# Seven block products for eight in the gate and up products of one token group, with two of the four weight sums made by DMA

## The chip, the cores and the metric

The kernel runs on one core of one Trainium2 chip. The metric is the device time of one execution in microseconds (us), as the median of several runs. Three runs of the kernel before gave 1436.48 us as the median (1433.87 to 1438.87).

## The reference, cut to what matters

One layer of a streaming encoder is computed for 1056 tokens: 1024 of a prompt and 32 of a running stream, with the same weights. Everything is float32. The part that the change touches is the feed-forward half:

```python
h = x * (1 + sc2) + sh2                                  # x: 1056 x 1024, after the first layer norm
y = (jax.nn.silu(h @ w_gate) * (h @ w_up)) @ w_down      # w_gate, w_up: 1024 x 2816; w_down: 2816 x 1024
x = _layer_norm(ALPHA * x + (1 + g2) * y, ln2_g, ln2_b)
```

## The kernel before, in words

Tokens lie along the free dimension, features along the partitions. The tokens are cut into two groups: group 0 has 512 and group 1 has 544 (`GN`). Each group is cut again into two halves (`MM`): 256 and 256, or 272 and 272. The 2816 hidden features are 22 tiles of 128; the 1024 input features are 8 blocks of 128 (`KT`).

Matrix products keep float32 accuracy by splitting both operands into a high and a low part of type float32r. `weights` (line 91) loads a block of weights of 128x1024 into a raw buffer, ScalarE casts it to the high part (line 102), and VectorE subtracts to get the low part (line 103). `gemm` (line 108) then runs three matmuls for each of the 8 input blocks: high by high (line 114), high by low (line 115) and low by high (line 116). There are three raw buffers (`RAW`), three for the high parts and three for the low parts (`WB`); the weights of all stages share them.

`up` (line 972) makes one tile of 128 hidden features for one group. It loads the tile's gate weights and its up weights, and for each half of the group runs the gate product and the up product, 24 matmuls each. Then ScalarE makes the sigmoid with three functions (lines 987 to 989), VectorE multiplies (lines 990 and 991), and the result is split into high and low (lines 992 and 993). One such tile of group 1 has 96 matmuls of 272 columns.

`down` (line 1011) takes a group of three or four such tiles (`GROUPS`) and adds their product with w_down into the residual `z`, for 8 blocks of 128 output features and two halves; `sublayer_end` (line 915) does the addition on VectorE (line 923). One tile more than the group has is made ahead of each `down`, so that the last tile's elementwise work is covered.

The order in `run` around the change: the tiles of group 0 come first, and among the last of them group 1's first layer norm is interleaved (`ln1`, line 930, which also writes the operand of group 1: `hh[1]` and `hl[1]`, high and low). Then `down(0, last)`, and `ln1_res` (line 947) on GpSimd. Then group 1: tiles 0 to 3, the last layer norm of group 0 (`ln2`, line 1025), `down` of tiles 0 to 2, tiles 4 to 6, `down`, tiles 7 to 10, `down`, and so on. The last group of tiles (19 to 21, with 18 made before) is done half by half: tiles 19, 20, 21 of the first half, `down`, `ln2`, and then the same for the second half, with the weights of the three tiles loaded and split a second time.

All loads and stores go through SyncE's queue in one order. The order of the instructions on each engine is fixed when the program is built, by a scheduler that follows the order of the code and what it expects to be ready.

Of the kernel before, what the change touches and what calls it, by code (L numbers as in the profile page):

```python
# [7 lines left out]
F32 = mybir.dt.float32  # L8
# [55 lines left out]
def f(ap):  # L64
    return ap.bitcast(F32)


class Kernel:
# [13 lines left out]
        return pool.tile(shape, dt, tag=tag, name=f"{self.phase}_{tag}_{self.n}", **kw)  # L82

    def load(self, out, in_):
        return self.nc.sync.dma_start(out, in_)

    def store(self, out, in_):
        self.nc.sync.dma_start(out, in_)
# [782 lines left out]

    def operand(self, c, pool):

        self.hh[c], self.hl[c] = ({a: self.t(pool, [P, KT, b - a], F32R, f"{x}{a}", 1) for a, b in MM[c]}
                                  for x in ("ah", "al"))

    def wo_mix(self, c, ks):
        self.phase = f"wo{c}"
# [51 lines left out]
    def ln1(self, c, st, a, b):  # L930
        self.phase = f"lna{c}"
        nc, z, hh, hl, sl = self.nc, self.z[c], self.hh[c][a], self.hl[c][a], slice(a, b)
        r, e = self.ln_stats(st, sl)
        for k in range(KT):
            yield
            self.phase = f"lna{c}"
            zk = z[:, k, sl]
            nc.vector.tensor_tensor(zk, zk, r, ALU.mult)
# [33 lines left out]
    def up(self, c, j, act, pool, cuts):  # L972
        self.phase = f"up{c}"
        nc, hh, hl = self.nc, self.hh[c], self.hl[c]
        ah, al = act[j] = [self.t(pool, [P, GN[c]], F32R, x, 5) for x in ("acth", "actl")]
        w = [self.weights(self.d["w_gu"][2 * j + i], KT, P) for i in range(2)]
        for a, b in cuts:
            ps = []
            for i in range(2):
                p = self.t((self.pg, self.pu)[i], [P, 512], F32, self.utag[i])[:, :b - a]  # L980
                self.gemm(p, w[i], slice(0, P), lambda k: hh[a][:, k], lambda k: hl[a][:, k])
                ps.append(p)
                if i == 0:
                    yield
                    self.phase = f"up{c}"
            s = self.t(self.p2, [P, 272], F32, "sil", 4)[:, :b - a]
            nc.scalar.activation(s, ps[0], AF.Exp, scale=-1.0)
            nc.scalar.activation(s, s, AF.Ln, bias=self.one)
            nc.scalar.activation(s, s, AF.Exp, scale=-1.0)
            nc.vector.tensor_tensor(s, ps[0], s, ALU.mult)  # L990
            nc.vector.tensor_tensor(s, ps[1], s, ALU.mult)
            nc.scalar.copy(ah[:, a:b], s)
            nc.vector.tensor_tensor(al[:, a:b], s, f(ah[:, a:b]), ALU.subtract)
            yield
            self.phase = f"up{c}"

    def last_weights(self, dst, units):

# [54 lines left out]
    def run(self):  # L1053
# [11 lines left out]
        self.dsf = t([8, 2, PAST + NS], "dsf")  # L1065
        self.dM = t([4, 9, P], "dM")
        self.dd0 = t([4, 9], "dd0")
        self.dmix = [t([P, KT, GN[c]], f"dmix{c}") for c in range(2)]
        self.pg = self.pool("pg", NB[0], space=PSUM)
        self.pt = self.pool("pt", NB[1], space=PSUM)  # L1070
# [124 lines left out]
        for g, (j0, nj) in enumerate(GROUPS):  # L1195
            if g == WOB:
                s4.close()
                s3.close()
                self.pu, self.utag = self.pool("pu", 3, space=PSUM), "gu"
                pb = self.pb = self.pool("pb", side="right")  # L1200
                weave(self.up(0, j0 + 1, act, pa, MM[0]))
                self.operand(1, pb)
                with tc.issue_after(self.lastz.ins):
                    self.wo_mix(1, self.KORDER)
                stb = self.ln_begin(nc.gpsimd)
                self.wo(1, stb, MM[1], nc.vector, pb)
                self.operand(1, pb)

                def norm():
                    for a, b in MM[1]:  # L1210
                        yield from self.ln1(1, stb, a, b)

                def fill():
                    for j in range(j0 + 2, j0 + nj):
                        yield from self.up(0, j, act, pa, MM[0])
# [12 lines left out]
        st.update(pivot=False, sum=True)  # L1228
        self.down(0, last, act, MM[0], st)
        self.ln1_res(1)  # L1230
        s5.close()
        pa = self.pool("pa1")
        act = {}
        for g, (j0, nj) in enumerate(GROUPS[:-1]):
            for j in range(j0 + (g > 0), j0 + nj + 1):
                weave(self.up(1, j, act, pa, MM[1]))
            if g == 0:
                for a, b in LN[0]:
                    self.ln2(0, st, a, b, "vpvvpvvp", "aaaaaaaa")
            st = self.ln_begin(nc.gpsimd, sum=False) if g == last - 1 else None  # L1240
            self.down(1, g, act, MM[1], st)
        st.update(pivot=False, sum=True, order=(4, 5, 6, 7, 0, 1, 2, 3))
        j0, nj = GROUPS[-1]

        n = nj * 256
        t = self.t(self.pz, [P, 4, n], F32R, "z0", 1)
        w = self.last_weights(((t[:, 0], t[:, 1]), (t[:, 2], t[:, 3])), (2, 3))
        act2 = dict(act)
        for half, (a, b) in enumerate(LN[1]):
            for j in range(j0 + 1 + (half and UPF), j0 + nj):  # L1250
                weave(self.up(1, j, (act, act2)[half], pa, ((a, b),)))
            if half == 0:
                h, l = (self.t(pb, [P, KT, b - a], F32R, f"{x}{a}", 1).rearrange("p k n -> p (k n)") for x in ("ah", "al"))
                for j in range(j0 + 1, j0 + 1 + UPF):
                    weave(self.up(1, j, act2, pa, (LN[1][1],)))
# [18 lines left out]
def _layout(inputs):  # L1274
# [21 lines left out]
    for n in ("ln1_g", "ln1_b", "ln2_g", "ln2_b"):  # L1296
# [16 lines left out]
    a["w_gu"] = units(np.stack([g["w_gate"][0].reshape(1024, 22, 128), g["w_up"][0].reshape(1024, 22, 128)],  # L1313
                               axis=2).reshape(1024, 5632), 128)
# [48 lines left out]
```

## Time and profile before

| | |
|---|---|
| median of 3 runs | 1436.48 us |
| the profiled execution | 1436.1 us, of which the span is 1434.3 us |
| TensorE (PE) busy | 1385.6 us, 97% of the span |
| VectorE (DVE) busy | 960.7 us, 67% |
| ScalarE (ACT) busy | 641.3 us, 45% |
| GpSimd (POOL) busy | 254.3 us, 18% |
| DMA | 205.49 MB on the one queue that the kernel uses |

PE's busy time is the time in which at least one matmul was in flight. Group 1's tiles and what follows them take the last 420 us of the span or so; the work of group 0 and of the mixers lies ahead of them.

### The profile page before, as it was taken

To read this page: it belongs to the slowest core of one execution; us is meant where nothing else is said; L and a number is where in the kernel's file an instruction comes from. 1 tells how busy PE (TensorE), PEld (TensorE's weight loads), DVE (VectorE), ACT (ScalarE), POOL (GpSimd) and SP (SyncE) were. 2 spreads that over 40 slices of the span, in tenths; PEclk is the share of its full clock that TensorE was granted. 3 is DMA by queue.
4 is the path that set the end of the run, shared out by engine and by line. 5 is a ranking of instruction groups with operands and counts; after the bars stand their busy time and mean duration, and the time that the engine had idled before them with its cause. 6 is when DMAs were issued, how large, how long until landed. Compare 5 with 4: busy or idle time off the path is not lost.

```text
span 1434.3 us, 28877 instructions
## 1 busy us (share of the span) xinstructions
PE 1385.6 (97%) x11141; PEld 1336.3 (93%) x11141; DVE 960.7 (67%) x2220; ACT 641.3 (45%) x1405; POOL 254.3 (18%) x295
## 2 busy tenths in 40 slices
PE   7999999999999899999999999999999999999994
PEld 4899988989899889999999998999999999999994
DVE  5558655678688777687767765668857545454676
ACT  3323244434445564546555353436745342424353
POOL 0103100043157300000000002254500000000433
PEclk9999999999999999999999999999999999999997
DMA  9754678565654755443443533522224222222431
GB/s 359 253 210 128 200 206 259 160 197 168 224 176 151 215 161 178 115 145 120 126 139 104 101 104 67 196 89 74 100 73 153 89 89 89 89 89 89 133 104 63
DMA packets 120867, 207.35 MB, mean 145 GB/s; under 512 B 21380, under 2 KB 76300, under 8 KB 120728
## 3 DMA queue, kind: packets, MB, share of 16 engines
q1 hardware_dynamic: 120728, 205.49, 45.9%
q8 instruction: 88, 1.44, 0.4%
q14 instruction: 51, 0.42, 0.1%
HBM read 173.78 MB, written 31.66 MB: 143 GB/s over the span
## 4 chain that ended last, share of the span: by engine, by line
PE 82%; DMA 7%; DVE 6%; ACT 1%; issue 1%; SPq 1%; POOL 1%; DVEq 0%; ACTq 0%; POOLq 0%
PE up_g L115 8%; PE up_g L116 8%; PE up_g L114 8%; PE dn_g L114 4%; PE dn_g L115 4%; PE dn_g L116 4%; PE up_u L116 3%; PE up_u L115 3%; PE up_u L114 3%; PE tm_g L279 2%; PE tm_g L280 2%; PE tm_g L281 2%; PE fox_t L729 2%; PE wo_g L114 2%; PE wo_g L115 2%; PE wo_g L116 2%
## 5 line engine op out<-in xcount | busy, mean ns | idle before, releaser
L114 PE MATMUL up_g<-wo_ah,up_whi 128*128 128x256 f32 (+1 forms) x1008 | 288.8, 287 | 3.4 <-ACT lna_tmp L942 3.3
L115 PE MATMUL up_g<-wo_al,up_whi 128*128 128x256 f32 (+1 forms) x1008 | 290.4, 288 | 0.4 <-DVE wo_al L945 0.4
L116 PE MATMUL up_g<-wo_ah,up_wlo 128*128 128x256 f32 (+1 forms) x1008 | 289.4, 287 | 0.0
L114 PEld LDWEIGHTS up_g<-wo_ah,up_whi 128*128 128x128 f32 x1008 | 191.4, 190 | 4.9 <-ACT wo_ah L944 3.5
L115 PEld LDWEIGHTS up_g<-wo_al,up_whi 128*128 128x128 f32 x1008 | 191.6, 190 | 1.3 <-DVE wo_al L945 0.7
L116 PEld LDWEIGHTS up_g<-wo_ah,up_wlo 128*128 128x128 f32 x1008 | 191.3, 190 | 0.4 <-DVE up_wlo L103 0.2
L102 ACT CAST up_whi<-up_raw 128x1024 fp32r<-128x1024 f32 x94 | 98.5, 1047 | 143.1 <-PE dn_u L115 53.8
L103 DVE TENSOR_TENSOR up_wlo<-up_raw,up_whi 128x1024 fp32r<-128x1024 f32 x94 | 121.1, 1288 | 61.0 <-ACT up_whi L102 60.7
L114 PE MATMUL dn_g<-up_acth,dn_whi 128*128 128x256 f32 (+1 forms) x464 | 133.8, 289 | 2.4 <-DVE mlstm_z L923 2.4
L115 PE MATMUL dn_g<-up_actl,dn_whi 128*128 128x256 f32 (+1 forms) x464 | 132.3, 286 | 0.0
L116 PE MATMUL dn_g<-up_acth,dn_wlo 128*128 128x256 f32 (+1 forms) x464 | 132.1, 285 | 0.0
L116 PE MATMUL up_u<-wo_ah,up_wlo 128*128 128x272 f32 (+1 forms) x400 | 115.4, 289 | 0.0
L114 PE MATMUL up_u<-wo_ah,up_whi 128*128 128x272 f32 (+1 forms) x400 | 114.9, 287 | 0.0
L115 PE MATMUL up_u<-wo_al,up_whi 128*128 128x272 f32 (+1 forms) x400 | 114.5, 286 | 0.0
L280 PE MATMUL tm_g<-tm_wlo,start_h1h 128*128 128x256 f32 (+1 forms) x384 | 111.3, 291 | 0.0
L281 PE MATMUL tm_g<-tm_whi,start_h1l 128*128 128x256 f32 (+1 forms) x384 | 111.0, 290 | 0.0
L279 PE MATMUL tm_g<-tm_whi,start_h1h 128*128 128x256 f32 (+1 forms) x384 | 110.3, 289 | 0.2 <-ACT tm_mixs L630 0.2
L114 PE MATMUL fm_g<-start_h1h,fm_whi 128*128 128x256 f32 (+2 forms) x344 | 102.7, 304 | 5.5 <-ACT fm_whi L102 1.9
L115 PE MATMUL fm_g<-start_h1l,fm_whi 128*128 128x256 f32 (+2 forms) x344 | 102.5, 298 | 0.1
L116 PE MATMUL fm_g<-start_h1h,fm_wlo 128*128 128x256 f32 (+2 forms) x344 | 101.4, 296 | 0.0
L114 PEld LDWEIGHTS dn_g<-up_acth,dn_whi 128*128 128x128 f32 x464 | 87.7, 189 | 3.3 <-DVE mlstm_z L923 3.0
L115 PEld LDWEIGHTS dn_g<-up_actl,dn_whi 128*128 128x128 f32 x464 | 87.8, 189 | 0.4
(447 smaller groups left out, 3806.2 us busy)
## 6 DMA issues: line engine op xcount, KB each, us to landing
up_raw<-w_gu SPq DMA_DIRECT2D x94, 512.0 KB
dn_raw<-w_dn SPq DMA_DIRECT2D x30, 512.0 KB
ada_late<-w_ada SPq DMA_DIRECT2D x24, 512.0 KB
wo_raw<-w_o SPq DMA_DIRECT2D x24, 512.0 KB
ada_araw<-w_ada SPq DMA_DIRECT2D x16, 512.0 KB
fm_raw<-w_in_f SPq DMA_DIRECT2D x16, 512.0 KB
tm_raw<-w_in SPq DMA_DIRECT2D x12, 512.0 KB
dn_raw<-w_dn SPq DMA_DIRECT2D x16, 384.0 KB
```

What stands on the lines that cost most here:

```text
L102: nc.scalar.copy(hi[:, :w], raw[:, :w])
L103: (eng or nc.vector).tensor_tensor(lo[:, :w], raw[:, :w], f(hi[:, :w]), ALU.subtract)
L114: nc.tensor.matmul(ps, hi, xh(k), start=start and k == 0, stop=False)
L115: nc.tensor.matmul(ps, hi, xl(k), start=False, stop=False)
L116: nc.tensor.matmul(ps, lo, xh(k), start=False, stop=stop and k == n - 1)
L279: nc.tensor.matmul(ps[:, :ncol], xh, hi, start=k == 0, stop=False)
L280: nc.tensor.matmul(ps[:, :ncol], xh, lo, start=False, stop=False)
L281: nc.tensor.matmul(ps[:, :ncol], xl, hi, start=False, stop=k == 7)
L729: nc.tensor.transpose(ps[:, y * P:(y + 1) * P], probs[y][:, b * P:(b + 1) * P], self.ident)
```

## The change

Group 1's tiles 4 to 20, seventeen of them, are made by a new function `sup` in the place of `up`. It treats the tile's product as a product of 2x2 blocks: gate and up by the lower and upper four input blocks on the side of the weights, the lower and upper four input blocks by the two halves of 272 tokens on the side of the operand. Seven block products with sums of blocks (the form of Strassen and Winograd) give the four results that eight block products gave. Each block product has four input blocks, so 12 matmuls.

- The sums on the operand's side are made once, by `sup_operand`, during group 1's tiles 0 and 1. It reads the operand back from DRAM, where `ln1` now stores it, and writes four sums of 128x4x272, split into high and low, into the buffers that held group 0's operand.
- Of the four sums of weights, two are made in DRAM by `sums`: SyncE copies the lower up block twice into a buffer `dp`, and one call later a DMA issued from GpSimd adds the lower gate block and the upper up block to it. There is one call of `sums` ahead of each of the last three tiles of group 0 or so, and one per tile of group 1 up to tile 15, so that a tile's sums are made some six tiles ahead of their use. The other two sums are two additions of 128x512 on VectorE in `sup`.
- A tile of `sup` loads 512 KB of gate weights, 512 KB of sums and 256 KB of up weights. It splits the gate weights, the two sums of its own, the two sums from DRAM, and the upper up block.
- The last layer norm of group 0 is divided: one half after tile 2, the other after tile 3.
- Tiles 19 and 20 are no longer done half by half; only tile 21 is.
- The buffers of the sigmoid are two of 544 columns for four of 272.

```diff
@@ load, ln1, up
     def load(self, out, in_):
-        return self.nc.sync.dma_start(out, in_)
+        self.lastload = self.nc.sync.dma_start(out, in_)
+        return self.lastload
...
+            if c:
+                self.store(self.dh[:, k, sl], h)
             nc.scalar.copy(hh[:, k], h)
             nc.vector.tensor_tensor(hl[:, k], h, f(hh[:, k]), ALU.subtract)
...
-            s = self.t(self.p2, [P, 272], F32, "sil", 4)[:, :b - a]
+            if a == cuts[0][0]:
+                sil = self.t(self.p2, [P, 544], F32, "sil", 2)
+            s = sil[:, a:b]
@@ new
+    def sums(self):
+        i = self.nsum
+        self.nsum += 1
+        blocks = lambda j: self.d["w_gu"][j].rearrange("p (b n) -> p b n", b=4)
+        if i < FF:
+            with self.tc.issue_after(self.lastload.ins):
+                self.store(self.dp[i], blocks(i)[:, 2:3].to_broadcast([P, 2, 512]))
+        if SJ <= i - 1 < FF:
+            self.nc.gpsimd.dma_start(self.dp[i - 1], blocks(i - 1)[:, 0:4:3], accum_op=ALU.add)
+
+    def sup_operand(self, ks):
...
+        for k in ks:
...
+            self.load(x, self.dh[:, k])
+            self.load(y, self.dh[:, k + 4])
+            tt(y[:, b], y[:, b], x[:, b], ALU.subtract)
+            tt(x[:, b], x[:, a], x[:, b], ALU.subtract)
+            tt(x[:, a], y[:, b], x[:, a], ALU.add)
+            tt(y[:, a], x[:, a], y[:, a], ALU.subtract)
+            for z, (h, l) in zip((x, y), self.T):
+                nc.scalar.copy(h[:, k], z)
+                tt(l[:, k], z, f(h[:, k]), ALU.subtract)
+            yield
+
+    def sup(self, j, act, pool):
...
+        raw = [self.t(self.wp, [P, 1056], F32, "raw", RAW)[:, :n] for n in (1024, 1024, 512)]
+        self.load(raw[0], self.d["w_gu"][j][:, :1024])
+        self.load(raw[1], self.dp[j].rearrange("p b n -> p (b n)"))
+        self.load(raw[2], self.d["w_gu"][j][:, 1536:])
...
+        w1 = big(raw[0])
+        tt(raw[0][:, lo], raw[0][:, lo], raw[1][:, hi], ALU.add)
+        tt(raw[0][:, hi], raw[0][:, hi], raw[0][:, lo], ALU.add)
+        w3 = big(raw[0])
+        w4 = big(raw[1])
+        w2 = split(*(self.t(self.px, [P, 544], F32R, x, 1)[:, :512] for x in ("w2h", "w2l")), raw[2])
...
+        nc.scalar.copy(u1, prod(w1[:4], own(0, 0)))
+        tt(x[:, a], prod(w1[4:], own(0, 4)), u1, ALU.add)
+        tt(uv[:, a], u1, prod(w3[:4], com(0)), ALU.subtract)
+        tt(uv[:, b], prod(w4[4:], com(1)), uv[:, a], ALU.add)
+        tt(x[:, b], prod(w3[4:], own(272, 4)), uv[:, b], ALU.add)
+        s = self.t(self.p2, [P, 544], F32, "sil", 2)
+        nc.scalar.activation(s, x, AF.Exp, scale=-1.0)
+        nc.scalar.activation(s, s, AF.Ln, bias=self.one)
+        nc.scalar.activation(s, s, AF.Exp, scale=-1.0)
+        tt(s, x, s, ALU.mult)
+        two = lambda y: y.rearrange("p (t n) -> p t n", t=2)
+        tt(two(c), prod(w4[:4], com(3)).unsqueeze(1).to_broadcast([P, 2, 272]), two(uv), ALU.add)
+        tt(c[:, a], prod(w2, com(2)), c[:, a], ALU.add)
+        nc.vector.scalar_tensor_tensor(c, c, -1.0, s, ALU.mult, ALU.mult)
+        nc.scalar.copy(ah, c)
+        tt(al, c, f(ah), ALU.subtract)
@@ run, group 1
+        operand = self.sup_operand(range(4))
+        for g, (j0, nj) in enumerate(GROUPS):
+            for j in range(j0 + (g > 0), min(j0 + nj + (g < last), FF - TS)):
+                if self.nsum <= FF:
+                    self.sums()
+                if j >= SJ:
+                    self.sup(j, act, pa)
+                    continue
+                if j == 2:
+                    weave(operand)
+                for _ in self.up(1, j, act, pa, MM[1]):
+                    if j < 2:
+                        next(operand, None)
+                if j >= 2:
+                    a, b = LN[0][j - 2]
+                    self.ln2(0, self.st0, a, b, "vpvvpvvp", "aaaaaaaa")
...
         for half, (a, b) in enumerate(LN[1]):
-            for j in range(j0 + 1 + (half and UPF), j0 + nj):
+            for j in range(FF - TS, FF):
                 weave(self.up(1, j, (act, act2)[half], pa, ((a, b),)))
```

`FF` is 22, `SJ` is 4 and `TS` is 1. The gate and up weights of a tile lie side by side in one row of `w_gu` now; a load still reads runs of 4 KB (2 KB for the upper up block).

More of the change, by code (lines that the diff above doesn't have):

```diff
@@ L48 @@
 WB = 3
+FF = 22
+SJ = 4
+TS = 1
 ALPHA = 2.0 ** 0.25
@@ L872, in operand @@
     def operand(self, c, pool):
-        self.hh[c], self.hl[c] = ({a: self.t(pool, [P, KT, b - a], F32R, f"{x}{a}", 1) for a, b in MM[c]}
-                                  for x in ("ah", "al"))
+        new = lambda tag, n: self.t(pool, [P, KT * 272], F32R, tag, 1)[:, :KT * n].rearrange("p (k n) -> p k n", k=KT)
+        self.hh[c], self.hl[c] = ({a: new(f"{x}{a}", b - a) for a, b in MM[c]} for x in ("ah", "al"))
     def wo_mix(self, c, ks):
@@ L975, in up @@
         ah, al = act[j] = [self.t(pool, [P, GN[c]], F32R, x, 5) for x in ("acth", "actl")]
-        w = [self.weights(self.d["w_gu"][2 * j + i], KT, P) for i in range(2)]
+        w = [self.weights(self.d["w_gu"][j][:, i * 1024:(i + 1) * 1024], KT, P) for i in range(2)]
         for a, b in cuts:
@@ L995, in up @@
             self.phase = f"up{c}"
+    def sums(self):
[8 more added lines that the diff above has]
+    def sup_operand(self, ks):
+        nc = self.nc
+        tt = nc.vector.tensor_tensor
+        if not self.T:
+            self.T = [[self.t(self.ph, [P, 2176], F32R, f"{x}{i}", 1).rearrange("p (k n) -> p k n", k=4)
+                       for x in ("ah", "al")] for i in (0, 256)]
+        a, b = slice(0, 272), slice(272, 544)
+        for k in ks:
+            self.phase = "sup"
+            x, y = ((self.t(self.px, [P, 544], F32, "c", 2) for _ in range(2)) if k % 2 else
+                    (f(self.t(self.px, [P, 544], F32R, z, 1)) for z in ("w2h", "w2l")))
+            self.load(x, self.dh[:, k])
[8 more added lines that the diff above has]
+            yield
@@ L1067, in run @@
         self.dd0 = t([4, 9], "dd0")
+        self.dh = t([P, KT, GN[1]], "dh")
+        self.dp = {j: t([P, 2, 512], f"dp{j}") for j in range(SJ, FF)}
+        self.T = []
+        self.nsum = SJ
         self.dmix = [t([P, KT, GN[c]], f"dmix{c}") for c in range(2)]
@@ L1211, in norm @@
                         yield from self.ln1(1, stb, a, b)
+                self.sums()
                 def fill():
                     for j in range(j0 + 2, j0 + nj):
+                        self.sums()
                         yield from self.up(0, j, act, pa, MM[0])
@@ L1233, in run @@
         act = {}
[L1234 to L1241, printed above, removed]
+        self.px = self.pool("px")
+        operand = self.sup_operand(range(4))
+        for g, (j0, nj) in enumerate(GROUPS):
+            for j in range(j0 + (g > 0), min(j0 + nj + (g < last), FF - TS)):
+                if self.nsum <= FF:
+                    self.sums()
+                if j >= SJ:
[9 more added lines that the diff above has]
+                    self.ln2(0, self.st0, a, b, "vpvvpvvp", "aaaaaaaa")
+            if g < last:
+                st = self.ln_begin(nc.gpsimd, sum=False) if g == last - 1 else None
+                self.down(1, g, act, MM[1], st)
         st.update(pivot=False, sum=True, order=(4, 5, 6, 7, 0, 1, 2, 3))
-        j0, nj = GROUPS[-1]
         n = nj * 256
@@ L1249, in run @@
         for half, (a, b) in enumerate(LN[1]):
-            for j in range(j0 + 1 + (half and UPF), j0 + nj):
+            for j in range(FF - TS, FF):
                 weave(self.up(1, j, (act, act2)[half], pa, ((a, b),)))
             if half == 0:
-                h, l = (self.t(pb, [P, KT, b - a], F32R, f"{x}{a}", 1).rearrange("p k n -> p (k n)") for x in ("ah", "al"))
-                for j in range(j0 + 1, j0 + 1 + UPF):
-                    weave(self.up(1, j, act2, pa, (LN[1][1],)))
+                h, l = (self.t(pb, [P, KT * 272], F32R, x, 1) for x in ("ah0", "al0"))
                 w.update(self.last_weights(((h[:, :n], l[:, :n]), (h[:, n:2 * n], l[:, n:2 * n])), (0, 1)))
```

28 lines of the change are left out of this document (26 added, 2 removed).

## The prediction

> **What bounds the kernel now.** I read the page first: busy time by engine, then the chain that ended last.
>
> ```profile
> span 1434.3 us, 28877 instructions
> PE 1385.6 (97%) x11141; PEld 1336.3 (93%) x11141; DVE 960.7 (67%) x2220; ACT 641.3 (45%) x1405; POOL 254.3 (18%) x295
> PE 82%; DMA 7%; DVE 6%; ACT 1%; issue 1%; SPq 1%; POOL 1%; DVEq 0%; ACTq 0%; POOLq 0%
> ```
>
> The matmuls end last; the other engines matter where they make them wait. Next the table of windows over group 1's part, with the borders put where tiles begin and end: 996 to 1014 holds the end of `down(0, last)`, then come tiles 0 to 3, `down` at 1062, tiles 4 to 6, `down` at 1117, tiles 7 to 10 from 1136, and so on. Columns: length, busy us (count) of PE, PEld, DVE, ACT, POOL, then clock, DMA share, GB/s.
>
> ```profile
> 996.00:1014.00 18.00, 18.00 (x155) 18.00 (x154) 17.93 (x36) 10.48 (x24) 13.61 (x15) 1.00 0.17 59
> 1014.00:1026.00 12.00, 12.00 (x98) 12.00 (x98) 12.00 (x23) 9.68 (x26) 10.54 (x10) 1.00 0.26 89
> 1026.00:1038.00 12.00, 12.00 (x99) 12.00 (x98) 7.62 (x14) 7.57 (x15) 0.00 (x0) 1.00 0.25 90
> 1038.00:1050.00 12.00, 12.00 (x98) 12.00 (x97) 4.99 (x9) 5.42 (x11) 0.00 (x0) 1.00 0.23 66
> 1050.00:1062.00 12.00, 12.00 (x97) 11.95 (x96) 4.48 (x9) 5.01 (x11) 0.00 (x0) 1.00 0.28 80
> 1062.00:1081.00 19.00, 19.00 (x149) 18.84 (x148) 18.31 (x45) 10.18 (x19) 2.44 (x3) 1.00 0.48 155
> 1081.00:1093.00 12.00, 12.00 (x98) 12.00 (x98) 11.03 (x25) 6.20 (x11) 2.44 (x3) 1.00 0.33 115
> 1093.00:1105.00 12.00, 12.00 (x98) 12.00 (x98) 6.75 (x11) 8.08 (x17) 0.00 (x0) 1.00 0.43 132
> 1105.00:1117.00 12.00, 12.00 (x98) 12.00 (x97) 4.67 (x9) 5.01 (x10) 0.00 (x0) 1.00 0.24 67
> 1117.00:1136.00 19.00, 19.00 (x153) 19.00 (x152) 13.27 (x30) 4.49 (x6) 0.00 (x0) 1.00 0.39 139
> 1148.00:1160.00 12.00, 12.00 (x98) 12.00 (x98) 5.00 (x9) 5.45 (x11) 0.00 (x0) 1.00 0.26 87
> 1208.00:1256.00 48.00, 48.00 (x386) 48.00 (x385) 19.80 (x33) 21.37 (x40) 0.00 (x0) 1.00 0.25 78
> 1256.00:1280.00 24.00, 24.00 (x193) 24.00 (x192) 13.67 (x28) 4.35 (x6) 0.00 (x0) 1.00 0.31 110
> 1409.00:1434.00 25.00, 6.83 (x49) 6.10 (x48) 16.86 (x42) 8.27 (x17) 9.41 (x11) 0.70 0.13 46
> ```
>
> PE has no gap here until 1409, at full clock. Four tiles, 4 x 96 matmuls, take 48 us: 0.125 us each. DVE is idle for more than half of a plain tile (5.00 of 12 us), but it is full at both ends of the ring of work around tile 0 (17.93 of 18, 12.00 of 12), where layer norms run.
>
> **What is removed.** A tile loses 12 of 96 matmuls. Seventeen tiles: 17 x 12 x 0.125 = 25.5 us, all of it on the path. A tile of `sup` takes PE 84 x 0.125 = 10.5 us. The sums themselves are no work of PE's.
>
> **What DVE gets in a tile.** Prices by form, of the phase 1136 to 1184 (the 768-column row from 1062 to 1117):
>
> ```profile
> L103 DVE TENSOR_TENSOR up_wlo<-up_raw,up_whi 128x1024 fp32r<-128x1024 f32 x6 | 7.4, 1226 | 9.1 <-ACT up_whi L102 9.1
> L103 DVE TENSOR_TENSOR dn_wlo<-dn_raw,dn_whi 128x768 fp32r<-128x768 f32 x4 | 3.8, 955 | 3.0 <-ACT dn_whi L102 3.0
> L990 DVE TENSOR_TENSOR up_sil<-up_g,up_sil 128x272 f32<-128x272 f32 x8 | 3.5, 442 | 8.4 <-ACT up_sil L989 8.0
> L102 ACT CAST up_whi<-up_raw 128x1024 fp32r<-128x1024 f32 x6 | 6.3, 1049 | 10.7 <-PE up_g L115 5.9 <-PE dn_u L115 3.5 <-PE up_u L115 1.3
> ```
>
> From 272 to 768 columns the price rises by 513 ns, 1.03 ns a column; so 512 columns are about 0.69 us and 544 about 0.72. A tile has three splits of 1024 (3.68), one split and two additions of 512 (2.07), five operations of 272 on products (2.21) and four of 544 (2.88): 10.8 us, against 5.00 before. That is more than PE's 10.5, but the durations overlap when DVE has a backlog:
>
> ```profile
> 1329.15 1.22 DVE L103 TENSOR_TENSOR dn_wlo<-dn_raw,dn_whi 128x1024 fp32r<-128x1024 f32 x1 [0.51 <-ACT dn_whi L102]
> 1330.29 0.43 DVE L993 TENSOR_TENSOR up_actl<-up_sil,up_acth 128x272 fp32r<-128x272 f32 x1
> 1330.64 1.19 DVE L923 SCALAR_TENSOR_TENSOR wo_z<-dn_g,start_mod,wo_z 128x272 f32<-128x272 f32 x3
> ```
>
> From start to start the split took 1.14 and not 1.22, the small one 0.35 and not 0.43. Fifteen operations at 0.08 less make 9.6 us of 10.5. In four tiles that is 38.4 to 43.2 us, and the two low parts of `down`'s weights that fall into such a stretch add 2.5, against 42 of PE. Of it the first tile's first two splits and the additions (2 x 1.23 + 2 x 0.69 = 3.8) can be done under the `down` ahead, where DVE has 10 of 24 us free, and the last tile's end (some 3 us) under the `down` behind. About 34 to 39 us must fit into 42. I take 1 us of waiting for each of the three stretches of four and for tiles 19 and 20: **4 us**, between 0 and 15; not below 0, since DVE gets work and no relief there.
>
> ACT's tile: three casts of 1.05, one of half that, the copy and four functions of 544: under 7.5 us of 10.5, so it is not the limit. PSUM's six banks cover a late evacuation.
>
> **The chain of weights.** With three raw buffers, and a tile that takes all three, a load waits until the tile before has split:
>
> ```profile
> SPq L85 <- DVE up_wlo L103: 186.2, 33, 8.6
> 1364.64 0.33 SPq L85 DMA_DIRECT2D up_raw<-w_gu  x1
> 1367.93 1.05 ACT L102 CAST up_whi<-up_raw 128x1024 fp32r<-128x1024 f32 x1 [1.60 <-DMA up_raw<-w_gu]
> ```
>
> Loads waited 186 us for that already. The second and third row are one load from issue to use, 3.3 us. The new loop is: the split of the third factor frees its raw buffer, load 3.3, cast 1.05, low part 1.23, two additions 1.38, cast 1.05, low part 1.23, and again: 9.2 us for each tile. It fits into 10.5 as long as a load takes under 4.6 us. I take nothing for it here; the second rival is about it.
>
> **The operand's sums and group 0's layer norm.** `sup_operand` has 16 operations of 272 and 8 of 544 on DVE, in tiles 0 and 1. There they run beside POOL (13.61 and 10.54 us busy), and rows of two operands in SBUF are dearer there:
>
> ```profile
> L938 DVE TENSOR_TENSOR wo_z<-wo_z,wo_pv 128x272 f32<-128x272 f32 x8 | 4.0, 574 | 0.0
> L835 DVE TENSOR_TENSOR wo_z<-wo_z,up_pv 128x272 f32<-128x272 f32 x2 | 3.5, 1734 | 3.5 <-ACT up_pv L834 3.5
> ```
>
> With 0.574: 16 x 0.574 + 8 x 0.72 = 15 us. From 996 to 1117 DVE was busy for 87.8 of 121 us (the sum of the nine rows above). Added are 15 and, for tiles 4 to 6, 3 x 5.8 = 17.4: 120.2, where PE now needs 121 - 4.5 = 116.5. So DVE is over by 3.7 us, less what goes into the `down` at 1117 (5.7 free) and plus what it waits. The move of the layer norm to tiles 2 and 3 helps, since there DVE had 14.5 us free. I take **4 us**, between 0 and 12. Who waits is PE, for the low parts of tiles 1 to 5, queued on DVE behind the operand's blocks of four and behind the layer norm's blocks of eight.
>
> **SyncE and GpSimd.** `ln1` issues 16 stores more, each waiting for ScalarE's row; the weights of `down(0, last)` and of tile 0 are queued behind them, and the 24 us of that `down` cover them. **1 us**, 0 to 4. Of each tile's copy and accumulation only the issue is on the queues. The accumulating DMA waits on GpSimd for a copy issued a call earlier, more than 10 us before; behind it stand the running sums of the layer norm, which nobody waits for in the tiles. The sums are ready some six tiles ahead. The trace has no accumulation and no copy in DRAM (one queue carries all); the nearest row is the load's 3.3 us, far below 60.
>
> **The end.** After the first half's `down`, PE had 18 + 12 us of work to cover the first half's `ln2`; now it has tile 21 and `down`, 6 + 12 = 18.
>
> ```profile
> 1382.96 0.13 PE dn_u L116
> ...
> 1394.14 4.06 DVE L1033 TENSOR_TENSOR wo_z<-wo_z,up_pv 128x272 f32<-128x272 f32 x8
> 1400.89 1.13 DVE L1034 TENSOR_TENSOR wo_z<-wo_z,up_qs 128x272 f32<-128x272 f32 x3
> ...
> 1408.37 0.14 PE dn_g L116
> 1408.54 2.76 DVE wo_z L923 x10
> ```
>
> In the trace that `ln2` lasted on DVE from the end of the first `down` on PE at 1383 to 1402, 19 us, but with four splits and three tiles' elementwise work in between (4 x 1.23 + 9 x 0.44 = 8.9), of which a third to a half stays. So 13 to 15 us against 18: it fits. From 1408.5 on DVE did the additions of the last `down`, in both versions after PE. **1 us**, from -1 (four splits and loads fewer) to 4.
>
> **Sum.** 4 + 4 + 1 + 1 = 10 us come back. The profiled execution took 1436.1 us (span 1434.3 and 1.8 around it), 0.4 under the median: 1436.1 - 25.5 + 10 = **1420.6 us**, 1.1% faster. Chance 0.50, and 0.10 for the case that nearly all is covered, 1411 to 1415.
>
> **Rival one: DVE is the bound from tile 0 to tile 6.** If DVE's operations there wait for POOL as L835's did (1734 ns for 442), the sixteen of the operand cost 16 x 1.3 = 21 us for the 2 that I took, or 19 more on an engine with no room, of which some 4 can be caught up: 15 us more than forecast, 1436 for the worst, and 1428 if half of them meet POOL. For it: DVE 12.00 of 12 beside POOL. Against: L938, in the same place, has 574, and POOL ends its work within tile 0. Chance 0.14. The Trainium skill's page "SBUF — State Buffer", section "Who interferes with whom", states that a VectorE instruction with two SBUF inputs and a GpSimd instruction that reads SBUF exclude each other for a whole instruction; by that rule each collision would cost up to GpSimd's duration, as L835's row bears out and L938's mean does not for most.
>
> **Rival two: loads become slow, and it ends slower than before.** A copy (512 KB) goes out right behind the last load, so ahead of the next tile's, and the accumulation shares the same engines. A tile's traffic grows from 1 MB in 12 us at a share of 0.25 to 1.25 MB of loads, 0.5 of copy and about 1 of accumulation in 10.5: a share near 0.8. With a copy and half an accumulation ahead a load takes 2.5 x 3.3 = 8.2 us; with the copy alone 6.6. The loop is then 14.1 or 12.5 us. It holds for the nine steps from one tile to the next within stretches while sums are issued (tiles 4 to 16): 9 x 2.0 = 18 or 9 x 3.6 = 32 us. With the forecast's 10: 1436.1 - 25.5 + 10 + 18 = 1438.6, or 1452.6; the middle is 1446. It decides from a load of 6.3 us on. For it: the share, and the lack of a fourth raw buffer. Against: a copy needs to meet the load just then, and there is 10.5 us for three of them. Chance 0.22. The Trainium skill's "DMA: Bandwidth & Descriptors", section "Issuing engines are not separate DMA queues", states that DMAs of all issuers run on the same 16 engines and interleave, which speaks against a sum that costs nothing; no run here shows it yet.
>
> **Rival three:** what is saved is lost to PE's own order (matmuls of 272 in the new order at more than 0.125, or the next tile's first product put behind the last), no change: 1436. Chance 0.04; a tile's windows of 12.00 us hold for any order here.
>
> **Numbers.** A measurement of this kernel can tell about 0.3%, 4.3 us, from no change. Faster by more (under 1432.2): the forecast 0.50, full cover 0.10, the milder part of rival one 0.08: 0.68. Within: the rest of rival one 0.06, rival three 0.04, the mild end of rival two 0.03: 0.13. Slower: the rest of rival two, 0.19. The range goes from full cover, 1410, to the lower half of rival two, 1442. The forecast's own range is 1415 to 1427.
>
> **What would show it.** PE's count falls by 204 matmuls. In the windows of tiles 7 to 18 a stretch of four takes 43 us with DVE at nine tenths; if it takes 47 or more with ScalarE's cast waiting for a DMA, it is rival two; if PE has its gaps before tile 7 and DVE is full there, rival one. The tail from PE's last matmul stays near 25 us. A stretch over 48 us would make the forecast wrong in sign.

## The result and the profile after

The changed kernel takes 1426.61 us, the median of 6 runs (1425.07 to 1432.34), beside 1435.32 us for the kernel before in the same measurement: a ratio of 0.9938, with a 95% interval of 0.992 to 0.9957. That is 8.7 us, or 0.6%, faster. The forecast was 1420.6 us in a range of 1410 to 1442: the sign and the range held, but of the 15.5 us that were to be gained from the profiled execution only some nine came.

The page of the changed kernel, in the lines that answer those of before:

```profile
span 1430.6 us, 28812 instructions
...
PE 1366.2 (96%) x10937; PEld 1312.7 (92%) x10937; DVE 1046.7 (73%) x2359; ACT 657.2 (46%) x1392; POOL 269.3 (19%) x313
...
PE 75%; DVE 10%; DMA 8%; ACT 3%; issue 2%; SPq 1%; POOL 0%; DVEq 0%; ACTq 0%
...
start_dp<-w_gu POOLq DMA_DIRECT2D x18, 512.0 KB, 7.1
```

The 204 matmuls are gone (11141 to 10937). The chain that ended last now leaves PE for a quarter of the span, where before it left it for 18%. The last line is new: one of the accumulating DMAs takes 7.1 us from issue to landing.

This profiled execution took 1432.34 us, 5.7 above the median of its kernel. Some 3 of them are lost ahead of 993 us, in work that is the same in both kernels: PE has 25 matmuls fewer there than in the repeat below, 14 of them in four microseconds in which its clock was granted at 0.58. A repeat of the same kernel, run with the experiments (1427.57 us, median of 8), was profiled at 1425.1 us. Its windows are used from here on; its span is 1423.3 us. Columns as before: length, busy us (count) of PE, PEld, DVE, ACT, POOL, clock, DMA share, GB/s. First the kernel before, in three stretches from 820 on, then the changed kernel with some of the same borders and finer ones.

```profile
820.00:993.00 173.00, 170.60 (x1409) 166.85 (x1409) 114.92 (x233) 77.15 (x169) 47.66 (x53) 0.99 0.36 107
993.00:1336.00 343.00, 343.00 (x2740) 342.63 (x2739) 193.81 (x366) 150.92 (x279) 32.83 (x32) 1.00 0.29 95
1336.00:1413.00 77.00, 77.00 (x610) 76.51 (x609) 57.32 (x102) 35.15 (x65) 32.17 (x31) 1.00 0.33 110
```

```profile
600.00:820.00 220.00, 220.00 (x1808) 218.29 (x1808) 169.75 (x430) 115.14 (x285) 4.09 (x9) 1.00 0.44 125
820.00:993.00 173.00, 169.83 (x1402) 166.24 (x1401) 116.56 (x231) 77.30 (x167) 51.05 (x57) 0.99 0.50 135
993.00:1336.00 343.00, 334.45 (x2653) 332.54 (x2652) 285.15 (x514) 168.05 (x273) 55.74 (x58) 1.00 0.58 162
1017.00:1065.00 48.00, 43.59 (x342) 42.83 (x341) 40.55 (x80) 28.12 (x61) 10.49 (x14) 1.00 0.72 187
1065.00:1107.00 42.00, 38.92 (x306) 38.42 (x305) 38.03 (x79) 23.75 (x40) 6.02 (x5) 1.00 0.70 195
1107.00:1204.00 97.00, 95.94 (x762) 95.49 (x761) 77.59 (x137) 43.28 (x59) 6.20 (x6) 1.00 0.66 176
1204.00:1246.00 42.00, 42.00 (x336) 41.96 (x336) 33.47 (x53) 19.53 (x28) 2.07 (x2) 1.00 0.60 156
1270.00:1312.00 42.00, 42.00 (x336) 42.00 (x336) 33.51 (x55) 21.02 (x30) 0.00 (x0) 1.00 0.35 114
1336.00:1402.00 66.00, 64.05 (x501) 62.81 (x499) 50.95 (x91) 33.31 (x56) 21.23 (x18) 1.00 0.29 93
```

What PE lost is read from its count, at 0.125 us a matmul. From 993 to 1336 it issued 2653 and not 2740: 87 fewer, 10.9 us. Of these, 72 are missing in tiles 0 to 6 and the `down` between them: 48 us from 1017 on hold 342 where 384 fit, 42 us from 1065 on hold 306 where 336 fit. Another 14 are missing from 1107 to 1204, 11 of them in the first stretch of four tiles (325 matmuls from 1136 to 1178). The two later stretches of four tiles (1204 and 1270) have 336 matmuls in 42 us, PE without a gap, and DVE with 8.5 us to spare. The DMA share is 0.66 to 0.72 where PE has its gaps.

A count from one profile is not exact. The first profile of the changed kernel has 32 matmuls fewer than the repeat in the same window, 4 us, though it is the same program:

```profile
993.00:1336.00 343.00, 332.86 (x2621) 330.28 (x2620) 280.48 (x506) 168.72 (x276) 49.52 (x52) 1.00 0.58 163
```

So what follows leans on the medians, and on counts only where several profiles agree.

Who waits there, and for what, is in the timeline of DVE around tile 0 and in the wait of PE that follows from it:

```profile
1015.54 1.32 DVE L951 TENSOR_TENSOR wo_al<-lna_tmp,wo_ah 128x272 fp32r<-128x272 f32 x2
1019.69 2.85 DVE L1035 TENSOR_TENSOR sup_w2l<-sup_w2l,sup_w2h 128x272 f32<-128x272 f32 x1 [2.83 <-DMA sup_w2l<-start_dh]
1022.57 0.44 DVE L1036 TENSOR_TENSOR sup_w2h<-sup_w2h 128x272 f32<-128x272 f32 x1
1022.93 1.22 DVE L107 TENSOR_TENSOR up_wlo<-up_raw,up_whi 128x1024 fp32r<-128x1024 f32 x1
...
1024.75 0.43 DVE L951 TENSOR_TENSOR wo_al<-lna_tmp,wo_ah 128x272 fp32r<-128x272 f32 x1
```

```profile
1025.24 0.39 PE L119 MATMUL up_g<-wo_al,up_whi 128*128 128x272 f32 x1 [3.21 <-DVE wo_al L951]
1045.51 0.39 PE L120 MATMUL up_u<-wo_ah,up_wlo 128*128 128x272 f32 x1 [1.12 <-DVE up_wlo L107]
```

DVE works in its order. The first sum of the operand (L1035) stands at its head and waits 2.83 us for the load of a block that `ln1` stored; behind it stand a low part of the weights (L107) and one of group 1's operand (L951), and PE waits 3.21 us for that one. The load is only half of it: the sum itself then took 2.85 us, where its like took 0.43 to 0.44, while GpSimd had rows of its own from 1018.58 to 1022.23 us.

### The profile page after: what moved, and what is told of

Same layout as the page of the kernel before. It is cut to its first block, busy times and chain, and to the rows that moved or that the text cites. A ratio compares the mean times of both kernels' runs of the same rounds, so it can differ in the third digit from the quotient of the medians.

```text
span 1430.6 us, 28812 instructions
## 1 busy us (share of the span) xinstructions
PE 1366.2 (96%) x10937; PEld 1312.7 (92%) x10937; DVE 1046.7 (73%) x2359; ACT 657.2 (46%) x1392; POOL 269.3 (19%) x313
## 3 DMA queue, kind: packets, MB, share of 16 engines
q0 software_dynamic: 4896, 9.44, 4.5%
## 4 chain that ended last, share of the span: by engine, by line
PE 75%; DVE 10%; DMA 8%; ACT 3%; issue 2%; SPq 1%; POOL 0%; DVEq 0%; ACTq 0%
PE up_g L119 5%; PE up_g L120 5%; PE up_g L118 5%; PE dn_g L118 4%; PE dn_g L119 3%; PE dn_g L120 3%; PE tm_g L283 3%; PE tm_g L284 3%; PE tm_g L285 3%; PE fm_g L118 3%; PE fm_g L119 2%; PE fm_g L120 2%; PE fox_t L733 2%; PE wo_g L120 2%; PE wo_g L118 2%
## 5 line engine op out<-in xcount | busy, mean ns | idle before, releaser
L119 PE MATMUL up_g<-wo_al,up_whi 128*128 128x256 f32 (+1 forms) x736 | 211.7, 288 | 3.8 <-DVE wo_al L951 3.8
L118 PE MATMUL up_g<-wo_ah,up_whi 128*128 128x256 f32 (+1 forms) x736 | 210.3, 287 | 3.9 <-ACT lna_tmp L946 3.3
L120 PE MATMUL up_g<-wo_ah,up_wlo 128*128 128x256 f32 (+1 forms) x736 | 210.4, 286 | 0.9 <-DVE up_wlo L107 0.9
L118 PEld LDWEIGHTS up_g<-wo_ah,up_whi 128*128 128x128 f32 x736 | 139.6, 190 | 5.4 <-ACT wo_ah L950 3.5
L119 PEld LDWEIGHTS up_g<-wo_al,up_whi 128*128 128x128 f32 x736 | 139.8, 190 | 5.0 <-DVE wo_al L951 4.2
L120 PEld LDWEIGHTS up_g<-wo_ah,up_wlo 128*128 128x128 f32 x736 | 139.7, 190 | 1.6 <-DVE up_wlo L107 1.4
L1057 ACT CAST sup_whi<-sup_raw 128x1024 fp32r<-128x1024 f32 x51 | 52.8, 1048 | 84.3 <-DVE sup_raw L1064 27.8
L107 DVE TENSOR_TENSOR up_wlo<-up_raw,up_whi 128x1024 fp32r<-128x1024 f32 x56 | 71.4, 1276 | 24.7 <-ACT up_whi L106 24.4
L1058 DVE TENSOR_TENSOR sup_wlo<-sup_raw,sup_whi 128x1024 fp32r<-128x1024 f32 x51 | 63.9, 1256 | 18.5 <-ACT sup_whi L1057 18.4
L118 PEld LDWEIGHTS fm_g<-start_h1h,fm_whi 128*128 128x128 f32 x344 | 65.4, 192 | 12.4 <-ACT start_h1h L223 3.1
L737 DVE TENSOR_TENSOR fox_ptl<-fox_t,fox_pth 128x256 fp32r<-128x256 f32 (+3 forms) x144 | 58.0, 417 | 23.7 <-ACT fox_pth L736 22.5
```

The source lines that it names most:

```text
L107: (eng or nc.vector).tensor_tensor(lo[:, :w], raw[:, :w], f(hi[:, :w]), ALU.subtract)
L118: nc.tensor.matmul(ps, hi, xh(k), start=start and k == 0, stop=False)
L119: nc.tensor.matmul(ps, hi, xl(k), start=False, stop=False)
L120: nc.tensor.matmul(ps, lo, xh(k), start=False, stop=stop and k == n - 1)
L737: nc.vector.tensor_tensor(pl[:, lo:nq], ps[:, lo:nq], f(ph[:, lo:nq]), ALU.subtract)
L1057: nc.scalar.copy(h, x)
```

## The experiments

Two theories were open for the 10.9 us. The first: the sums' DMAs crowd the loads, and engines that work in order wait for data (the second rival's mechanism, in another place). The second: it is the operand, by the order of DVE's work or by its number. Every kernel below is the changed one with the edit shown. The first four ran beside 1436.72 us for the kernel before, the next four beside 1437.29, the last two beside 1438.89, and the first measurement beside 1435.32; so ratios are compared. PE's matmuls between fixed borders, from each kernel's windows, show the place (the kernel before has 2740 and 1809 there):

| kernel | median us | ratio, 95% interval | 993 to 1336 | missing, us | 600 to 820 |
|---|---|---|---|---|---|
| changed kernel, first measurement | 1426.61 | 0.9938 [0.992, 0.9957] | 2621 | 14.9 | 1806 |
| repeat of the changed kernel | 1427.57 | 0.9929 [0.9903, 0.9954] | 2653 | 10.9 | 1808 |
| no operand's sums | 1424.91 | 0.9914 [0.9881, 0.9948] | 2660 | 10.0 | 1809 |
| no DMAs for the sums | 1420.30 | 0.9878 [0.985, 0.9906] | 2703 | 4.6 | 1808 |
| operand one tile later | 1426.03 | 0.9912 [0.9882, 0.9942] | 2629 | 13.9 | 1805 |
| neither sums' DMAs nor operand | 1417.67 | 0.9854 [0.9832, 0.9877] | 2723 | 2.1 | 1809 |
| sums early | 1421.97 | 0.9896 [0.9873, 0.9919] | 2701 | 4.9 | 1786 |
| copies, no accumulation | 1419.87 | 0.9876 [0.9857, 0.9895] | 2691 | 6.1 | 1810 |
| sums early, operand later | 1421.69 | 0.9892 [0.9872, 0.9913] | 2700 | 5.0 | 1778 |
| a plain copy for the accumulation | 1424.86 | 0.988 [0.9837, 0.9924] | 2669 | 8.9 | 1809 |
| sums early, no operand | 1421.90 | 0.9877 [0.985, 0.9904] | 2725 | 1.9 | 1789 |

**The repeat** was run with no edit.

> The changed kernel once more, for a second profile. In its first profiled execution (1432.3 us, 5.7 above the median) the clock was 0.58 at 880 to 884 us and 0.86 near 1050. Theory A (the loss sits in tiles 0 to 2 and is there in every execution): PE waits again about 3 us for group 1's low operand and 2 us for a low part of weights, near 1025 and 1050; the low clock at 880 is gone and the span is nearer to 1425. Theory B (loads grow slow by the sums' DMAs): waits for DMA in the tiles of sup again, PE below 42 us of work in 42 us in stretches of four.

It gave the same time within the intervals, and the profile above. The wait of 3.2 us near 1025 is there again, the second one is 1.12 us for 2, the low clock at 880 is gone, and of the stretches of four the first alone is short.

**No operand's sums.** `ln1` stores nothing for them, the generator is empty, and the common products take plain blocks.

```diff
-            if c:
-                self.store(self.dh[:, k, sl], h)
...
-        operand = self.sup_operand(range(4))
+        operand = iter(())
```

> Leaves out the sums on the operand's side: ln1 does not store, sup_operand does not run, and the products take unsummed blocks of the operand in their place (so the output is another function). All matmuls stay. Theory A (the loss is in tiles 0 to 2, from the operand's loads and its 24 operations on VectorE): 8 to 10 us less than the changed kernel, 1417 to 1419, no wait of PE from 1015 to 1060. Theory B (slow loads): 1 to 3 us less, 1424 to 1426, and the waits from 1084 on stay.

One of its six runs took 2917.27 us; the median and the ratio are those of the other five. The median gains 2.7 us on the repeat, with overlapping intervals, and the window from 993 to 1336 seven matmuls, 0.9 us. The 8 to 10 us that the second theory asks for did not come: as long as the sums' DMAs are there, the operand isn't what most of the loss hangs on.

**No DMAs for the sums.** No call of `sums`; the second load of a tile reads 512 KB of plain weights.

```diff
-        self.load(raw[1], self.dp[j].rearrange("p b n -> p (b n)"))
+        self.load(raw[1], self.d["w_gu"][j][:, 1024:])
...
-                self.sums()
```

> Leaves out the two sums of weights made in DRAM: no copies and no accumulating DMAs; sup loads the up weights, unsummed, in the place of the sums (so the output is another function). Same loads, same splits, same matmuls. Theory A: 1 to 3 us less than the changed kernel, 1424 to 1426; the wait near 1025 stays, perhaps shorter. Theory B (the sums' traffic on the 16 engines slows the loads): 6 to 12 us less, 1415 to 1421, and ScalarE no longer waits for loads in the tiles of sup.

```profile
993.00:1336.00 343.00, 339.92 (x2703) 338.61 (x2702) 288.14 (x523) 169.52 (x274) 45.71 (x44) 1.00 0.38 119
1017.00:1065.00 48.00, 46.34 (x361) 45.50 (x360) 42.89 (x87) 31.11 (x67) 8.72 (x9) 1.00 0.39 117
1107.00:1204.00 97.00, 97.00 (x775) 97.00 (x774) 78.62 (x138) 42.65 (x59) 0.00 (x0) 1.00 0.37 117
```

These are its windows. 50 matmuls are back, 6.3 us, and the median is 7.3 us lower; the share at 1017 falls from 0.72 to 0.39, and from 1107 to 1336 PE has no gap. DVE has all its work here, the operand too (42.89 busy of 48): so its number of operations alone isn't the cause. One part of the expectation was missed: ScalarE still waits for weights in the tiles of `sup`, eight times and 22.6 us in total (nine times and 33.2 us on the repeat).

**Operand one tile later.** The blocks of the operand start in tile 1, where `ln1`'s rows are done.

```diff
-                    if j < 2:
+                    if j == 1:
```

> Computes everything; the operand's four parts are put into tile 1 instead of tile 0, one after each product. Theory A, in the form that VectorE stands still in order for a load from DRAM (3.8 us) in front of what PE needs: the wait of 3.2 us for the low operand goes, and with it the drop of the clock behind it: 4 to 7 us less than the changed kernel, 1420 to 1423. If it is the amount of VectorE's work around tiles 0 to 6 and not its order: no change within 1.5 us. Theory B: no change.

No change in the time: 1426.03 beside 1427.57 us, inside the intervals. From 1017 to 1065 it had 359 matmuls for 342, but 290 for 306 in the next 42 us, at a clock of 0.96, and 182 for 204 in the 24 us ahead: the gaps moved. The order alone isn't the cause, and the second theory falls as the main one.

**Neither** (the edits of the two kernels without operand and without DMAs together).

> Leaves out both kinds of sums by extra traffic: the operand's sums (unsummed blocks in their place) and the two sums of weights in DRAM (the up weights in their place); another function, the same matmuls, loads and splits in sup. If the two costs are separate, their gains add: 6 to 7 us and 2 to 4 us less than the changed kernel, so 1416 to 1419, and PE has no gap over 1.5 us between 1000 and 1340. If they are one cost (the same full stretch of VectorE and of the DMA engines), the sum is not more than the larger, about 1420.

```profile
993.00:1336.00 343.00, 341.58 (x2723) 340.78 (x2722) 281.23 (x504) 167.80 (x270) 46.35 (x44) 1.00 0.35 111
```

With both gone PE is short of 17 matmuls, 2.1 us, and the median is 19.6 us under the kernel before. Beside the kernel without DMAs alone, 20 matmuls (2.5 us) or 3.2 us of the medians' gains are the operand's. So of the 10.9 us the sums' DMAs make 6.3, the operand 2.5, and 2.1 are the new order itself: the waits of tile 4's first products, 1.4 us on a cast. The shares of the first two hold in this order of taking away; the operand taken away first gave 0.9 us, and the DMAs then 7.9, so part of the loss needs both.

**Sums early.** The calls start with group 0's tile 4, so that the last are made within group 0.

```diff
+                if j >= 4:
+                    self.sums()
                 weave(self.up(0, j, act, pa, MM[0]))
```

> Computes everything; the copies and the accumulating DMAs go out one per tile of group 0 from tile 4 on, so that nearly all are done before group 1 begins. Theory C (the sums' traffic costs because it meets the operand's loads and the weights' loads in group 1's tiles 0 to 10): 4 to 7 us less than the changed kernel, 1420 to 1423, near the kernel without these DMAs. Rival (the traffic costs wherever it is, and the mixers' loads wait for it now): no change or slower, 1427 to 1433, with new waits of PE for DMA between 480 and 880.

```profile
600.00:820.00 220.00, 217.98 (x1786) 215.77 (x1786) 167.34 (x424) 113.16 (x279) 13.70 (x19) 1.00 0.67 171
993.00:1336.00 343.00, 339.92 (x2701) 338.43 (x2700) 289.06 (x522) 172.24 (x281) 45.74 (x45) 1.00 0.38 120
```

The window after 993 is as good as without the DMAs (2701 and 2703), while 22 matmuls, 2.8 us, are missing in group 0's tiles, where the DMAs now run (share 0.67 for 0.44). PE has two waits there that the repeat has not, 0.39 us for a load and 1.63 us for VectorE. This kernel computes all that the changed one does. It beats the kernel before by 1.0%, and its ratio is 0.0033 under the changed kernel's, though the two intervals overlap by 0.0016.

**Copies, no accumulation.** GpSimd issues nothing; SyncE's copies stay.

```diff
-        if SJ <= i - 1 < FF:
-            self.nc.gpsimd.dma_start(self.dp[i - 1], blocks(i - 1)[:, 0:4:3], accum_op=ALU.add)
```

> Leaves out the accumulating DMAs and keeps the copies (the sums lack two blocks: another function). If the copy on SyncE's queue, right ahead of the next tile's loads, is what makes loads late: within 2 us of the changed kernel, 1425 to 1429. If it is the accumulation on the engines: 4 to 7 us less, 1420 to 1423.

The ratio, 0.9876, is that of the kernel without either DMA (0.9878), and PE has 12 matmuls fewer, 10 of them from 1017 to 1065, where the clock was 0.96. The copies cost little by themselves; the second DMA is the dear one.

**Sums early, operand later** (both edits).

> Computes everything; the sums of weights early as in e5, and the operand's parts in tile 1 as in e3. Theory C: with the engines free, the operand's loads come in time wherever its parts are put, so this is within 1.5 us of e5. If VectorE's order around tile 0 costs by itself: 2 to 4 us less than e5, 1417 to 1420.

As sums early alone (1421.69 and 1421.97): with the traffic gone from tiles 0 to 6, the operand's place makes no difference either.

**A plain copy for the accumulation.**

```diff
-            self.nc.gpsimd.dma_start(self.dp[i - 1], blocks(i - 1)[:, 0:4:3], accum_op=ALU.add)
+            self.nc.gpsimd.dma_start(self.dp[i - 1], blocks(i - 1)[:, 0:4:3])
```

> The DMA that GpSimd issues for a tile's sums stays, with its wait for the copy, its place and its 512 KB, but it copies the two blocks and doesn't add them to what the first copy wrote; so what the tiles load is no sum, and the kernel computes another function. Without any second DMA the time was 1419.9 us, with the accumulating one 1427.6. If it is the accumulation (it has to read what it adds to, so moves more, and landed after 7 us and more) that crowds the loads out, a plain copy costs a part of that: the time comes out near 1422 (1420 to 1424), with 766 to 776 matmuls from 1107 to 1204 where the changed kernel had 762 and the kernel without the second DMA 775. If it is any second DMA, or GpSimd's wait for the copy and what is queued behind it there, the time stays near 1427 (1425 to 1429), with some 762 matmuls there.

The queue of GpSimd's DMAs on the page of the repeat, and then on this kernel's page, with its issues:

```profile
q0 software_dynamic: 4896, 9.44, 4.5%
```

```profile
q0 software_dynamic: 2592, 9.44, 2.2%
...
start_dp<-w_gu POOLq DMA_DIRECT2D x18, 512.0 KB, 4.8
```

For the same 9.44 MB the accumulation took twice the time of the 16 engines (4.5% against 2.2% of the span) and landed after 7.3 us on the repeat's page, not 4.8. The two cases' signs disagree. The time, 1424.86 us, falls between their ranges. The ratio, 0.988, is that of no second DMA (0.9876), but its interval, 0.9837 to 0.9924, holds most of what lies between the two. From 1107 to 1204 the count is 774, as the first case has it. That the accumulating DMAs cost time is shown (0.9929 with them and 0.9876 without, intervals apart), and that they take more of the DMA engines than a plain copy; how much of the time comes of their being accumulations isn't settled by the medians.

**Sums early, no operand.**

> The sums issued early, as before, and in addition no store of the operand and no sums of it: the common products of the tiles take the plain blocks of the operand, so the kernel computes another function. With the sums early and the operand the time was 1422.0 us; with neither sums' DMAs nor operand 1417.7. If the early sums are free and the rest of the difference is the operand's 32 operations of VectorE and its loads, this one comes out at 1417.7 (1416 to 1419.5), with 383 matmuls from 1017 to 1065 as in the kernel before. If the early sums have a price of their own under group 0's tiles, it stays near 1420 to 1422, with fewer matmuls somewhere ahead of 993.

The window from 993 to 1336 is as full (2725) as with neither, and yet the time stays at 1421.90 us, as the second case has it. By the ratio it lies between sums early and neither (0.9877, for 0.9896 and 0.9854), and its interval meets both. What decides is the place: all three kernels with early sums lack matmuls from 600 to 820 (1786, 1778 and 1789, where the others have 1805 to 1810), 2.5 to 3.8 us. Early sums have a price of their own.

**How the sums' DMAs cost PE its time.** The counts of all profiles in three windows separate what the medians don't (the kernel before has 383, 335 and 776):

| kernel | 1017 to 1065 | 1065 to 1107 | 1107 to 1204 |
|---|---|---|---|
| changed kernel, first profile | 320 (clock 0.96) | 305 | 753 |
| repeat | 342 | 306 | 762 |
| no operand's sums | 364 | 307 | 762 |
| operand one tile later | 359 | 290 (clock 0.96) | 758 |
| a plain copy for the accumulation | 344 (clock 0.96) | 308 | 774 |
| copies, no accumulation | 351 (clock 0.96) | 320 | 775 |
| no DMAs for the sums | 361 | 322 | 775 |
| neither | 383 | 320 | 776 |
| sums early | 364 | 320 | 775 |
| sums early, operand later | 363 | 320 | 774 |
| sums early, no operand | 385 | 321 | 776 |

From 1107 to 1204 only the four profiles with accumulating DMAs there are short, by 12 matmuls or more, 1.5 us; the plain copy is not. Weights come late there. The first load of a tile, from its issue on SyncE to the cast that waits for it, on the repeat and then without the sums' DMAs:

```profile
1149.53 0.34 SPq L88 DMA_DIRECT2D sup_raw<-w_gu  x1
1156.25 1.05 ACT L1057 CAST sup_whi<-sup_raw 128x1024 fp32r<-128x1024 f32 x1 [4.09 <-DMA sup_raw<-w_gu]
```

```profile
1156.36 0.33 SPq L88 DMA_DIRECT2D sup_raw<-w_gu  x1
1159.57 1.05 ACT L1057 CAST sup_whi<-sup_raw 128x1024 fp32r<-128x1024 f32 x1 [1.59 <-DMA sup_raw<-w_gu]
```

It took 6.7 us and 3.2. PE's waits for such a cast came to 1.07 us on the repeat (at 1175). This is the first theory's mechanism, and here it is the accumulation's.

From 1065 to 1107 the five profiles in which GpSimd issues a DMA there are short by some 14 matmuls, 1.75 us, whether it accumulates or not. Slow loads are not what PE waits for in this window. The repeat, and then two rows without the sums' DMAs:

```profile
1081.28 1.04 POOL L1019 DMA_DIRECT2D start_dp<-w_gu  x1
1081.96 2.92 DVE L1058 TENSOR_TENSOR sup_wlo<-sup_raw,sup_whi 128x1024 fp32r<-128x1024 f32 x1
1086.08 0.61 DVE L927 SCALAR_TENSOR_TENSOR wo_z<-dn_g,start_mod,wo_z 128x240 f32<-128x240 f32 x2
1086.84 0.37 PE L118 MATMUL sup_g<-wo_ah,sup_whi 128*128 128x272 f32 x1 [1.66 <-ACT mlstm_z L1139]
```

```profile
1078.18 1.35 DVE L1058 TENSOR_TENSOR sup_wlo<-sup_raw,sup_whi 128x1024 fp32r<-128x1024 f32 x1
1081.27 0.61 DVE L927 SCALAR_TENSOR_TENSOR wo_z<-dn_g,start_mod,wo_z 128x240 f32<-128x240 f32 x2
```

The low part of tile 4's weights (L1058) took 2.92 to 3.18 us in these five, beside GpSimd's DMA issue and the layer norm's rows that follow it there, and 1.35 or 1.36 in the six others. Behind it on VectorE stands the addition that empties a PSUM bank, the place where a product's results stand, for PE's next product (L927), and that product waits 1.4 to 2.1 us in the five profiles, and in none of the others. The view names a row of ScalarE as the releaser. But the product started 0.15 us after that addition's end in the repeat, and as long after it without the DMAs (at 1082.03 us), so the addition is the likelier one.

From 1017 to 1065 both the operand and the DMAs cost, and several things mix. VectorE waited 2.83 us for the operand's load, but that load was no slower than without the DMAs: 2.94 us from issue to use (1016.75 to 1019.69), and 2.92 (1014.18 to 1017.10). It went out later: ahead of it in SyncE's queue stand a copy for the sums and two of `ln1`'s stores, and without the DMAs one store. Then the sum took 2.85 us beside GpSimd, and 0.50 without the DMAs. Only the smaller wait, 1.12 us at 1045, stands behind a slow load (5.3 us from issue to use, 3.4 without the DMAs). No run takes these apart further, and none tells whether it is GpSimd's DMA issue or the changed time of its other rows that VectorE meets.

## Why the prediction was right in sign and too large

**The gross gain** held: 204 matmuls, and 10.5 us for a tile (336 matmuls in 42.00 us). The prices did too: additions of 512 at 0.68 to 0.71 us, operations of 544 at 0.72.

**Step that failed: the sums' DMAs.** "Of each tile's copy and accumulation only the issue is on the queues", with 1 us for all of SyncE and GpSimd, and the load's 3.3 us taken as the nearest row for an accumulation. An accumulation took 7.1 us and twice a plain copy's engine time, and in place of 1 us the pair cost 6.3 (by the windows) to 7.3 (by the medians). That they are ready long before their use, which is true, says nothing of what they do to the loads beside them, to the order of SyncE's queue, and to VectorE beside the engine that issues them. "PSUM's six banks cover a late evacuation" failed in one place with it: PE waited 1.66 us at 1086.84, most likely for a bank that VectorE emptied late. The second rival had one of the mechanisms, at nearly its price for a load (6.7 us, for 6.6 to 8.2), but took it to hold PE up at every tile. The share in the stretches of four was 0.60 and not 0.8, and of ScalarE's waits for loads PE noticed 1.07 us:

```profile
ACT sup_w2h L1057 <- DMA sup_raw<-w_gu: 18.4, 4, 6.3
ACT sup_whi L1057 <- DMA sup_raw<-w_gu: 14.8, 5, 4.2
```

These are the repeat's waits (total us, times, longest): nine waits for weights, 33.2 us, the rest covered by what PE still had. In tiles 0 to 6 the operand's loads, `ln1`'s stores, the sums and the layer norm's rows on GpSimd come together, and less covers them. The Trainium skill's page "DMA: Bandwidth & Descriptors", section "Issuing engines are not separate DMA queues", states that DMAs of all issuers share the same 16 engines. The loads from 1107 to 1204 agree with it, 6.7 us with accumulating DMAs beside them and 3.2 without; the wait of 1.66 us does not come of it.

**The stretches of four** were taken at 4 us, for VectorE. The two later ones cost nothing that the windows show (1204 and 1270); the first cost 11 matmuls, 1.4 us, by late weights. DVE was busy 8.4 us a tile (33.5 of 42), under the 9.6 to 10.8 that were worked out, and it had room.

**The operand and the layer norm**, taken at 4 us, came out near that, 2.5 for the operand and 2.1 for the rest, and that is in part luck: the rest is tile 4's wait for a cast and not the layer norm. The reason given was half right: DVE is the engine that holds PE up, but waiting for a load and slowed beside GpSimd, and not for the number of its operations.

**The end** was taken at 1 us, up to 4, and cost 3.6. PE had 1.9 us of gaps from 1336 to the end of its last product, where before had none (77.00 of 77). Then the tail, of which the prediction said that it stays near 25 us, as it counted from 1409, where the last `down` was still running: the last product and the sums after it, in the kernel before, and then in the repeat.

```profile
1414.36 0.28 PE L116 MATMUL dn_u<-up_acth,up_al 128*128 128x272 f32 x1
1416.98 0.72 PE L854 MATMUL lnb_t<-up_zs,start_onesm 128*128 128x272 f32 x2 [2.34 <-POOL up_zs L845]
```

```profile
1401.64 0.28 PE L120 MATMUL dn_u<-up_acth,up_al 128*128 128x272 f32 x1
1405.73 0.87 PE L858 MATMUL lnb_t<-sup_zs,start_onesm 128*128 128x272 f32 x2 [3.81 <-POOL sup_zs L849]
```

From the last product to the end it was 19.9 us before (1434.3 - 1414.36) and is 21.7 now (1423.3 - 1401.64). The additions of the last `down` come later after their products, so the running sums do, and PE's statistics wait 3.81 us for them and not 2.34. The first half's layer norm has less cover, as that step feared, and the additions queue behind it: DVE's last row of it (L1137) starts at 1398.87 in the timeline.

**The sum** closes by profile: 25.5 less 10.9, less 3.6 for the end, less 0.9 from 820 to 993, where PE has 1402 for 1409 matmuls, is 10.1 of the 11.0 us between the two spans. The remaining 0.9 lies ahead of 820, where PE was ten matmuls further (6383 for 6373), in work that is the same in both. This is the sum of the repeat's profile; the first profile's window is 4 us worse.

**The first rival** is refuted as a bound: on the repeat the operand's additions of 272 took 0.43 to 0.44 us, but for one of 2.85 beside POOL. Its mechanism is real all the same. That one addition (2.4 us longer) and tile 4's low part (2.92 us for 1.35) stand in front of the two longest waits of PE, which the prediction's "DVE is over by 3.7 us" doesn't hold. **The third** is refuted by the full stretches.

## What to carry to other kernels

A DMA that nobody waits for still has a price. Loads beside it land later, it changes what stands ahead of a load in the queue, and the engine that issues it may meet another engine's operations. The price is paid where an engine that works in order stands still with other work behind it. Ask for each added transfer what share the DMA engines have in that stretch, what loads run there, who stands behind those loads, and what runs beside the issuing engine. A transfer that can run early belongs into a stretch with a low share, and even there (from 0.44 to 0.67) it cost 2.5 to 3.8 us here. A plain load is no measure for an accumulating DMA.

## What was not expected of the hardware

An accumulating DMA of 512 KB within DRAM took twice the engine time of a plain one (4.5% and 2.2% of the span for 9.44 MB) and 1.9 times the packets (4896 and 2592). The bytes that the two pages count are the same (9.44 MB on that queue).

A VectorE split of 1024 columns took 2.92 to 3.18 us where GpSimd issued a DMA and worked on rows of the layer norm beside it, in all five profiles, and 1.35 or 1.36 where GpSimd issued none, in all six.

PE's clock falls for a while at places that differ between executions of one program. In the first profile of the changed kernel it was 0.58 from 880 to 884 us, where the repeat had full clock (22 and 36 matmuls):

```profile
880.00:884.00 4.00, 4.00 (x22) 3.88 (x21) 2.08 (x7) 0.74 (x3) 0.00 (x0) 0.58 0.13 22
```

```profile
880.00:884.00 4.00, 4.00 (x36) 3.95 (x34) 2.13 (x8) 1.55 (x3) 0.00 (x0) 1.00 0.13 19
```

Such stretches are one reason why one profile's windows are good to some 4 us only: so far apart are the two profiles of the changed kernel between 993 and 1336.
